# Two pacing tables of a two-layer transformer step changed: when VectorE gathers the w_ada products in the feed-forward stage, and how densely layer 0's weight sums are made in DRAM

## The chip, the cores and the metric

The kernel runs on one core of a Trainium2 chip. A core has a matrix engine (TensorE: PE in the profile, with its weight loads shown apart as PEld), VectorE (DVE), ScalarE (ACT), GpSimd (POOL) and SyncE (SP), which here only issues DMA transfers. Each engine works through its own instructions in order and waits on semaphores for the others; 16 DMA engines move data between DRAM and on-chip memory. The metric is the device time of one execution in microseconds (us).

## The reference, cut to what matters

Two trunk layers are run over 640 tokens (128 context, 512 latent), with model width 1024 and feed-forward width 2816, all in float32.

```python
def trunk_layer(x, mod, ...):
    sh1, sc1, g1, sh2, sc2, g2 = jnp.split(mod, 6, axis=-1)     # mod = silu(c) @ w_ada[l] + b_ada[l]
    h = rms_norm(x, g_pre[0]) * (1 + sc1) + sh1
    qa, ka, va, qb, kb, vb, uc, gates = combined_projection(h, w_in_l)
    oa, ob = attend(qa, ka, va, qb, kb, vb)
    oc = fourier_mix(uc)
    y = merge_branches(oa, ob, oc, gates, w_branch_l, w_out_l)  # sigmoid(gate) * (o @ w_branch), summed, @ w_out
    x = x + g1 * rms_norm(y, g_post[0])
    h = rms_norm(x, g_pre[1]) * (1 + sc2) + sh2
    x = x + g2 * rms_norm(swiglu(h, w_ffn_in_l, w_ffn_out_l), g_post[1])
```

`mod` needs, for each layer, a product of one vector with the 1024 x 6144 matrix `w_ada[l]`; its six parts are needed at different places, and the kernel computes them as six "rounds".

## The kernel before, in words

**Weights.** Every weight tile (512 KB: 128 x 1024 floats) is loaded by SP into one of 4 `wraw` buffers (`pump`, L168; halves for pairs of products L164) and then split into two float32r parts: ACT writes `whi` (L172), DVE writes `wlo`, the rest (L173). A product is three matmuls: hi by hi, hi by lo, lo by hi. SP takes the loads in order, each as soon as a buffer comes free.

**A planned clock.** The program is written out by hand in one order. `vt` adds up the planned TensorE time of what has been written so far (columns at 2.4 GHz; real time is longer, as the attention's own work is not counted). `step(dur)`, called after each product, writes side work into the program when `vt` has reached its time: the DRAM sums, the w_ada steps and the attention ticks. So two tables decide where in each engine's order the side work stands; nothing is decided at run time.

**The stages of a layer.** First the projections, Fourier mixing and attention; then the gates of branch B with the last merges (`merge(1, n)`), where TensorE also computes w_ada rounds (`ADA_MIX`: three rounds in layer 0, two in layer 1; weights through the same 4 `wraw` buffers, L492); then `out_proj`; then the feed-forward (`ffn`) in three parts of 6, 8 and 8 column blocks. Each part is a run of **pairs** (4, 8 and 8 of them) and then an **output product**. A pair (`pair`) computes two column blocks with seven half-size products (12 matmuls of 320 columns each). Its partial results leave PSUM through ACT (L750, L758) and DVE (L754, L764, L768, L773) into three `tmp` buffers, which ACT, DVE and POOL (L765) work on; then the gate function runs (L1536 to L1542). The output product (`xstat`; L1397 to L1399) multiplies the activations by `w_ffn_out`, one 512 KB unit after another: 6 units in part 1, 8 in part 2, 30 matmuls of 512 columns each; results are gathered on ACT in part 1 (L1578) and on DVE in part 2 (L1580). Part 3 ends in another form, `xstat_tiles`.

**w_ada in the feed-forward.** Four rounds in layer 0 and one in layer 1 run here on DVE (`ada_round` with `acc`). A round has 8 loads of 512 KB into three `ada_side` buffers (SP, L153; the next load is written right behind the step that frees its buffer) and 16 DVE steps over 128 x 1024 floats (L498 for the first load, L500 after that), two per load; then three empty steps (`ADA_LAG`), and a last one in which TensorE adds up over partitions (L512). `step` writes one DVE step each time `ada_acc` has gathered `ada_dt`.

**Sums in DRAM.** The half-size products need four sums of blocks of `w_ffn_in`, made wholly in DRAM (`sum_jobs`): 96 jobs a layer, each over 256 rows. Copies go through SP (L412), additions through POOL's DMA queue (L415), and a copy of a sum waits for the addition before it. Job i of layer 0 is written at planned time `SUM_START + i * SUM_DT[0]`; layer 1's jobs are paced by `SUM_DT[1]` from layer 0's feed-forward on.

Of the kernel before, what the change touches and what calls it, by code (L numbers as in the profile page):

```python
# [34 lines left out]
ADA_FFN = ([(0, 5), (1, 0), (1, 1), (1, 2)], [(1, 5)])  # L35
FFN_PARTS = (6, 8, 8)
SUMS_AT = (0.1, 0.2, 2.0, 3.0, 4.0, 5.0, 9.0, 99.0)
SUM_START, SUM_DT, SUM_ROWS = 20.0, (3.6, 7.5), 256
TICK = 2.5
ADA_DT, ADA_LAG = 4.2, 3  # L40
T_TOK, T_KO, T_V = 2.7, 0.9, 2.9
ADA_D0 = 2.1
T_COL, T_OUT, T_GM = 8.0, 5.2, 2.0
# [244 lines left out]
class Kernel:  # L288
# [1221 lines left out]
    def ffn(self, l):  # L1510
        nc = self.nc
        n0 = 0
        while self.sums_due:
            self.sums_due.popleft()()
        if l + 1 < L:
            self.sums_due, self.sums_at, self.sums_dt = deque(self.sum_jobs(l + 1)), self.vt, SUM_DT[1]
        for p, nt in enumerate(FFN_PARTS):
            last = p == len(FFN_PARTS) - 1
            aT = [self.fp.tile([128, 4, T], F32R, name=f"aT{i}", tag=f"mt{i}", bufs=1) for i in range(4)]

            def split_of(j, aT=aT):

                return tuple(aT[i + j // 4][:, j % 4, :] for i in (0, 2))

            def lhs(j, t, split_of=split_of):
                return tuple(self.cut(w, t) for w in split_of(j))
            gate = {}

            def evac(kind, n, gate=gate, split_of=split_of, n0=n0):
                def f(src, g):  # L1530
                    c0, c1 = HALVES[g]
                    if n not in gate:
                        gate[n] = self.fp.tile([128, T], F32, name="sg", tag="sg", bufs=2)
                    t = gate[n][:, c0:c1]
                    if kind == "fg":
                        nc.scalar.activation(t, src, AF.Tanh, scale=0.5)  # L1536
                        nc.vector.scalar_tensor_tensor(t, t, 1.0, src, op0=OP.add, op1=OP.mult)
                        return
                    nc.vector.tensor_tensor(t, t, src, op=OP.mult)  # L1539
                    hi, lo = (w[:, c0:c1] for w in split_of(n - n0))  # L1540
                    nc.scalar.activation(hi, t, AF.Copy, scale=0.5)
                    nc.vector.scalar_tensor_tensor(lo, t, 0.5, hi.bitcast(F32), op0=OP.mult, op1=OP.subtract)  # L1542
                return f

            first = n0
            if p == 0:
                first = FFN_SINGLE
                seq = [(kind, n) for n in range(first) for kind in ("fg", "fu")]
                self.tmp = [self.fp.tile([128, 320], F32, name=f"tmp{i}") for i in range(3)]
                for g in range(2):  # L1550
                    self.run_tasks(GTOK[g])
                    if g:
                        self.sums(self.z, SUMS_AT)
                    for kind, n in seq[:3]:
                        self.proj((l, kind, n), g, evac(kind, n), 4, HALVES)
                self.W.alt.clear()
                for kind, n in seq[3:]:
                    self.proj2((l, kind, n), evac(kind, n), HALVES)
                self.run_tasks(("sums",))
                rounds = ADA_FFN[l]  # L1560
                self.run_tasks(range(5))
                side = self.fp.tile([128, 5, D], F32, name="ada_side", tag="x", bufs=1)
                self.W.side_open([side[:, i, :] for i in range(2, 5)], 8 * len(rounds))
                self.ada = self.ada_rounds(rounds, side[:, 0:2, :])
                self.ada_acc, self.ada_dt = 0.0, ADA_DT
            half = (n0 + nt - first) // 2
            for n in range(first, first + half):
                for kind in ("fg", "fu"):
                    ev = [evac(kind, n + i * half) for i in range(2)]
                    self.pair(("pair", l, kind, n, n + half), lambda i, src, g: ev[i](src, g))  # L1570
            if p == 0:
                y = self.fix.tile([128, 5, D], F32, name="y", tag="os", bufs=1)
            keys = [[((l, "fo", h, n0 + k), k) for k in range(0, nt, 2)] for h in range(2)]
            if not last:
                def acc_y(t, h, ps, p=p):
                    d = y[:, t, 512 * h:512 * h + 512]
                    if p == 0:
                        nc.scalar.activation(d, ps, AF.Copy)  # L1578
                    else:
                        nc.vector.tensor_tensor(d, d, ps, op=OP.add)  # L1580
                self.xstat(keys, lhs, acc_y)
            else:
                self.ada_finish()
                self.alt_pieces()
                gm = self.load_gm(l, 1)
                self.x = self.fp.tile([128, 5, D], F32, name="x", tag="x", bufs=1)
                for t in range(5):
                    nc.sync.dma_start(self.x[:, t, :], self.xmid[t * 128:t * 128 + 128])

                def done(t, h, ps):  # L1590
                    c = slice(512 * h, 512 * h + 512)
                    d = y[:, t, c]
                    nc.vector.tensor_tensor(d, d, ps, op=OP.add)
                    self.square(t, h, d)

                    def scale():
                        (nc.vector if h else nc.gpsimd).tensor_tensor(d, d, gm[:, min(t, 1), c], op=OP.mult)
                    if h == 0 and t in GTOK[1]:
                        self.defer(T_GM, scale, ("gm", t))
                    else:  # L1600
                        scale()
                    if h == 1:
                        self.run_tasks((("gm", t),))
                        self.tail(l + 1, 0 if l + 1 < L else None, t, y[:, t, :])
                self.xstat_tiles(keys, lhs, done)
            n0 += nt
# [129 lines left out]
```

## Time and profile before

| | |
|---|---|
| Time, median of 3 runs | 2187.17 us (2185.57 to 2188.48) |
| Profiled execution: its own time | 2188.79 us |
| Profiled execution: span from first to last instruction | 2187.0 us |
| Busy share of the span | PE 96%, PEld 89%, DVE 58%, ACT 42%, POOL 23% |
| Mean granted TensorE clock (1 is 2.4 GHz) | 0.992 |

TensorE is nearly always busy, so time is saved only where it waits or where its clock is low. The other engines' shares are means over stages that differ.

### The profile page before, as it was taken

The page shows a single profiled execution, that of the slowest core. Times are in us where ns is not written, and L with a number is a line of the kernel's source. Part 1 is how long each engine was busy: PE and PEld are TensorE (multiplying, and loading weights), DVE is VectorE, ACT ScalarE, POOL GpSimd, SP SyncE. Part 2 cuts the span into 40 slices and gives each one's busy share as a digit, 9 for nine tenths or more (in the row PEclk, how much of TensorE's full clock was granted, in tenths as well). Part 3 has the DMA queues.
Part 4 walks back from the last instruction along what each step waited for, and adds up shares of the span by engine and source line. Part 5 has one row for each costly group of instructions (what it writes and reads, how often), then busy time and mean ns, then how long its engine had stood idle before and what let it go on. Part 6 is the DMA issues. An engine that isn't in the chain of part 4 may idle for free.

```text
span 2187.0 us, 36116 instructions
## 1 busy us (share of the span) xinstructions
PE 2109.1 (96%) x13876; PEld 1944.0 (89%) x13876; DVE 1272.2 (58%) x2377; ACT 910.0 (42%) x1944; POOL 510.8 (23%) x783
## 2 busy tenths in 40 slices
PE   6999999999899998999999999999999999999998
PEld 4999999998778888889879999999989898998996
DVE  3555565552247858668765556555433687573773
ACT  3644444432245344324345544434323543441451
POOL 3112335432224111102142112243321320010012
PEclk9999999999899999999999999999999999999999
DMA  7443477778864767668856334555565344442443
GB/s 271 137 97 89 110 177 191 176 190 251 237 205 138 211 178 200 179 198 222 248 165 161 88 96 104 132 131 128 130 184 203 124 136 143 123 150 86 135 149 121
DMA packets 369804, 349.69 MB, mean 160 GB/s; under 512 B 16608, under 2 KB 294144, under 8 KB 369376
## 3 DMA queue, kind: packets, MB, share of 16 engines
q1 hardware_dynamic: 337040, 293.51, 42.6%
q0 software_dynamic: 32160, 53.63, 14.9%
q8 instruction: 109, 1.79, 0.3%
q14 instruction: 63, 0.52, 0.1%
q10 hardware_dynamic: 432, 0.25, 0.0%
HBM read 335.50 MB, written 95.72 MB: 197 GB/s over the span
## 4 chain that ended last, share of the span: by engine, by line
PE 55%; DVE 7%; ACT 3%; issue 3%; DMA 1%; POOL 1%; DVEq 0%; ACTq 0%; SPq 0%; POOLq 0%
PE ps_mm L741 15%; PE ps_mm L647 7%; PE ps_mm L648 6%; PE ps_mm L649 6%; PE ps_mm L1397 5%; PE ps_mm L1398 5%; PE ps_mm L1399 5%; PE ps_o L849 1%; DVE wlo L173 1%; DVE ada_side L500 1%; PE ps_t L836 1%; ACT whi L172 1%; DVE sg L1539 1%; PE ps_s L809 1%; PE ps_s L810 1%
## 5 line engine op out<-in xcount | busy, mean ns | idle before, releaser
L173 DVE TENSOR_TENSOR wlo<-wraw,whi 128x512 fp32r<-128x512 f32 (+1 forms) x453 | 405.7, 901 | 394.5 <-ACT whi L172 389.2
L647 PE MATMUL ps_mm<-hT_hi,whi 128*128 128x256 f32 (+2 forms) x1552 | 491.8, 317 | 11.7 <-ACT whi L172 10.1
L649 PE MATMUL ps_mm<-hT_hi,wlo 128*128 128x256 f32 (+2 forms) x1552 | 483.5, 312 | 2.8 <-DVE wlo L173 2.8
L648 PE MATMUL ps_mm<-hT_lo,whi 128*128 128x256 f32 (+2 forms) x1552 | 483.0, 311 | 0.0
L172 ACT ACTIVATE whi<-wraw 128x512 fp32r<-128x512 f32 (+1 forms) x453 | 354.0, 790 | 305.6 <-PE ps_mm L1399 126.5
L647 PEld LDWEIGHTS ps_mm<-hT_hi,whi 128*128 128x128 f32 x1552 | 294.3, 190 | 22.2 <-ACT whi L172 12.5
L649 PEld LDWEIGHTS ps_mm<-hT_hi,wlo 128*128 128x128 f32 x1552 | 293.9, 189 | 4.9 <-DVE wlo L173 4.9
L648 PEld LDWEIGHTS ps_mm<-hT_lo,whi 128*128 128x128 f32 x1552 | 294.2, 190 | 0.4
L741 PE MATMUL ps_mm<-S,whi 128*128 128x320 f32 x960 | 214.1, 311 | 8.1 <-DVE tmp L754 8.1
L741 PE MATMUL ps_mm<-hT_hi,whi 128*128 128x320 f32 x640 | 199.8, 312 | 14.7 <-ACT tmp L750 14.7
L741 PE MATMUL ps_mm<-hT_hi,wlo 128*128 128x320 f32 x640 | 198.5, 310 | 0.0
L741 PE MATMUL ps_mm<-hT_lo,whi 128*128 128x320 f32 x640 | 198.4, 310 | 0.0
L765 POOL TENSOR_TENSOR tmp<-tmp,tmp 128x320 f32<-128x320 f32 x40 | 52.9, 1323 | 590.7 <-DVE tmp L764 482.9
L741 PEld LDWEIGHTS ps_mm<-S,whi 128*128 128x128 f32 x960 | 160.5, 189 | 11.3 <-DVE tmp L754 11.2
L1397 PE MATMUL ps_mm<-whi,aT 128*128 128x512 f32 x400 | 158.2, 395 | 0.0
L1399 PE MATMUL ps_mm<-whi,aT 128*128 128x512 f32 x400 | 157.9, 395 | 0.0
L1398 PE MATMUL ps_mm<-wlo,aT 128*128 128x512 f32 x400 | 157.8, 394 | 0.0
L741 PE MATMUL ps_mm<-S,wlo 128*128 128x320 f32 x480 | 148.3, 309 | 0.0
L741 PEld LDWEIGHTS ps_mm<-hT_hi,whi 128*128 128x128 f32 x640 | 120.9, 189 | 19.0 <-ACT tmp L750 17.3
L741 PEld LDWEIGHTS ps_mm<-hT_lo,whi 128*128 128x128 f32 x640 | 121.0, 189 | 0.1
L741 PEld LDWEIGHTS ps_mm<-hT_hi,wlo 128*128 128x128 f32 x640 | 121.1, 189 | 0.0
L1333 ACT ACTIVATE sg<-ps_mm 128x384 f32<-128x384 f32 x96 | 41.7, 435 | 190.3 <-PE ps_mm L649 190.2
(236 smaller groups left out, 3998.9 us busy)
## 6 DMA issues: line engine op xcount, KB each, us to landing
wraw<-in_w_in SPq DMA_DIRECT2D x92, 512.0 KB, 4.7
wraw<-wsum SPq DMA_DIRECT2D x160, 256.0 KB, 3.4
wsum<-in_w_ffn_in POOLq DMA_DIRECT2D x64, 512.0 KB, 6.9
wraw<-in_w_ffn_in SPq DMA_DIRECT2D x120, 256.0 KB, 3.8
wraw<-in_w_ada SPq DMA_DIRECT2D x56, 512.0 KB, 6.1
wraw<-in_w_ffn_out SPq DMA_DIRECT2D x44, 512.0 KB, 3.6
ada_side<-in_w_ada SPq DMA_DIRECT2D x40, 512.0 KB, 4.8
wsum<-in_w_ffn_in SPq DMA_DIRECT2D x32, 512.0 KB, 5.2
```

The lines of the kernel that those rows point to most:

```text
L172: self.k.nc.scalar.activation(hi, src, AF.Copy)
L173: self.k.nc.vector.tensor_tensor(lo, src, hi.bitcast(F32), op=OP.subtract)
L500: nc.vector.scalar_tensor_tensor(acc[:, s, :], u.raw, c, acc[:, s, :], op0=OP.mult, op1=OP.add)
L647: nc.tensor.matmul(ps, wh, xh[:, c0:c1], start=(k == 0), stop=False)
L648: nc.tensor.matmul(ps, wh, xl[:, c0:c1], start=False, stop=False)
L649: nc.tensor.matmul(ps, wl, xh[:, c0:c1], start=False, stop=(k == K - 1))
L741: nc.tensor.matmul(ps, w[p][:, k, :], x[q][:, k, :], start=first and k == 0 and j == 0, stop=last and k == 3 and j == 2, skip_group_check= ...
L765: nc.gpsimd.tensor_tensor(m5, m5, m1, op=OP.subtract)
L1333: lambda ps, g: self.nc.scalar.activation(sg[:, GROUPS[g][0]:GROUPS[g][1]], ps, AF.Tanh, scale=0.5))
L1397: nc.tensor.matmul(ps, xh, u.hi[:, i, :], start=st and i == 0, stop=False)
L1398: nc.tensor.matmul(ps, xh, u.lo[:, i, :], start=False, stop=False)
L1399: nc.tensor.matmul(ps, xl, u.hi[:, i, :], start=False, stop=sp and i == 1)
```

## The change

Layer 0's sums start at planned time 5.0 and come every 2.9, where they started at 20.0 and came every 3.6. A w_ada step in the feed-forward is written every 8.0 of planned time in the pairs and every 1.8 in the output products of parts 1 and 2, where it was every 4.2 throughout.

```diff
-SUM_START, SUM_DT, SUM_ROWS = 20.0, (3.6, 7.5), 256
+SUM_START, SUM_DT, SUM_ROWS = 5.0, (2.9, 7.5), 256
 TICK = 2.5
-ADA_DT, ADA_LAG = 4.2, 3
+ADA_DT, ADA_LAG = (8.0, 1.8), 3
...
-                self.ada_acc, self.ada_dt = 0.0, ADA_DT
+                self.ada_acc, self.ada_dt = 0.0, ADA_DT[0]
...
+                self.ada_dt = ADA_DT[1]
                 self.xstat(keys, lhs, acc_y)
+                self.ada_dt = ADA_DT[0]
```

Worked out from the tables: the last of layer 0's sums was written at planned time 363, after the gates and last merges (293 to 357), and now at 284, ahead of them.

**VectorE in a pair** (layer 0, part 2, the second pair). Rows from the middle of it, before; `tmp`, `sg` and `aT` are the pair's own tiles, `wlo` a weight split, `ada_side` a w_ada step:

```order
L173 TENSOR_TENSOR wlo_272<-wraw,whi_271 128x512
L500 SCALAR_TENSOR_TENSOR ada_side<-ada_side,ada_st 128x1024
L173 TENSOR_TENSOR wlo_272<-wraw,whi_271 128x512
L1539 TENSOR_TENSOR sg<-sg,ps_mm 128x320
L1542 SCALAR_TENSOR_TENSOR aT_7803<-sg,aT_7801 128x320
L173 TENSOR_TENSOR wlo_270<-wraw,whi_269 128x512
L764 TENSOR_TENSOR tmp_6661<-ps_mm,tmp_6661 128x320
L173 TENSOR_TENSOR wlo_270<-wraw,whi_269 128x512
L500 SCALAR_TENSOR_TENSOR ada_side<-ada_side,ada_st 128x1024
L768 TENSOR_TENSOR tmp_6662<-ps_mm,tmp_6662 128x320
```

The same place of the changed kernel:

```order
L173 TENSOR_TENSOR wlo_272<-wraw,whi_271 128x512 x2
L500 SCALAR_TENSOR_TENSOR ada_side<-ada_side,ada_st 128x1024
L1539 TENSOR_TENSOR sg<-sg,ps_mm 128x320
L1542 SCALAR_TENSOR_TENSOR aT_7826<-sg,aT_7824 128x320
L173 TENSOR_TENSOR wlo_270<-wraw,whi_269 128x512
L764 TENSOR_TENSOR tmp_6661<-ps_mm,tmp_6661 128x320
L173 TENSOR_TENSOR wlo_270<-wraw,whi_269 128x512
L768 TENSOR_TENSOR tmp_6662<-ps_mm,tmp_6662 128x320
```

Of two steps in these rows one is left. Over the eight pairs of part 2 the steps that work on DVE go from 18 to 8.

**VectorE at the end of part 2's output product** (layer 0), its last two units and the start of the first pair of part 3; `y` rows gather the product's results. Before:

```order
L173 TENSOR_TENSOR wlo_272<-wraw,whi_271 128x512 x2
L500 SCALAR_TENSOR_TENSOR ada_side<-ada_side,ada_st 128x1024
L1580 TENSOR_TENSOR y<-y,ps_mm 128x512 x5
L173 TENSOR_TENSOR wlo_270<-wraw,whi_269 128x512 x2
L500 SCALAR_TENSOR_TENSOR ada_side<-ada_side,ada_st 128x1024 x2
L173 TENSOR_TENSOR wlo_268<-wraw,whi_267 128x512
L754 TENSOR_TENSOR tmp_6661<-ps_mm,tmp_6662 128x320
```

The same place of the changed kernel:

```order
L500 SCALAR_TENSOR_TENSOR ada_side<-ada_side,ada_st 128x1024 x3
L1580 TENSOR_TENSOR y<-y,ps_mm 128x512 x5
L173 TENSOR_TENSOR wlo_270<-wraw,whi_269 128x512 x2
L500 SCALAR_TENSOR_TENSOR ada_side<-ada_side,ada_st 128x1024 x4
L173 TENSOR_TENSOR wlo_268<-wraw,whi_267 128x512
L754 TENSOR_TENSOR tmp_6661<-ps_mm,tmp_6662 128x320
```

Three steps instead of one stand ahead of the last gathering, and four instead of two ahead of the first pair's L754. At the first unit of part 1's output product six stand in a row, elsewhere in the output products two to four.

**SyncE in the gates of layer 0** (a piece of the difference; `wsum` rows are the DRAM sums):

```order
 L168 DMA wraw<-in_w_in 128x8x128
 L168 DMA wraw<-in_w_ada 128x1024 x3
-L412 DMA wsum_97<-wsum_96 256x512
-L168 DMA wraw<-in_w_branch 128x4x256
-L168 DMA wraw<-in_w_ada 128x1024
-L412 DMA wsum_97<-wsum_96 256x512
+L168 DMA wraw<-in_w_branch 128x4x256
+L168 DMA wraw<-in_w_ada 128x1024
 L168 DMA wraw<-in_w_in 128x8x128
 L168 DMA wraw<-in_w_ada 128x1024 x2
```

The copies are gone from here; they, and POOL's additions with them, stand further ahead, among the attention's loads. Between the weight loads nothing else moved.

## Rows read from the trace of the kernel before

**Rows 1.** The page: busy time, share of the span and instructions.

```profile
PE 2109.1 (96%) x13876; PEld 1944.0 (89%) x13876; DVE 1272.2 (58%) x2377; ACT 910.0 (42%) x1944; POOL 510.8 (23%) x783
```

**Rows 2.** Waits of PEld, whole run: us in total, times, longest.

```profile
PEld ps_mm L741 <- ACT tmp L750: 17.3, 10, 3.2
...
PEld ps_mm L741 <- DVE tmp L754: 11.2, 12, 1.1
```

**Rows 3.** Waits of PEld in layer 0's gates, 503.21 to 601.8 us.

```profile
PEld ps_mm L647 <- ACT whi L172: 10.7, 3, 3.9
...
PEld ps_mm L649 <- DVE wlo L173: 3.0, 4, 1.0
```

**Rows 4.** Windows, gates: length; PE, PEld, DVE, ACT, POOL busy; clock; DMA share; GB/s.

```profile
503.21:601.80 98.59, 87.45 (x627) 73.29 (x628) 23.60 (x39) 20.04 (x35) 22.73 (x32) 0.93 0.87 252
...
1601.01:1677.20 76.19, 75.42 (x564) 67.13 (x565) 23.06 (x39) 19.84 (x35) 15.35 (x20) 1.00 0.60 180
```

**Rows 5.** Timeline, PEld in layer 0's gates: start, length, instruction, [idle before].

```profile
548.19 0.19 PEld L647 LDWEIGHTS ps_mm<-hT_hi,whi 128*128 128x128 f32 x1 [3.92 <-ACT whi L172]
...
586.70 0.29 PEld L647 LDWEIGHTS ps_mm<-hT_hi,whi 128*128 128x128 f32 x1 [3.28 <-ACT whi L172]
```

**Rows 6.** Timeline, SP in layer 0's gates.

```profile
540.24 0.38 SPq L168 DMA_DIRECT2D wraw<-in_w_in  x1
...
555.73 0.38 SPq L168 DMA_DIRECT2D wraw<-in_w_in  x1
```

**Rows 7.** Timeline, ACT in layer 0's gates.

```profile
547.08 1.06 ACT L172 ACTIVATE whi<-wraw 128x1024 fp32r<-128x1024 f32 x1 [7.75 <-DMA wraw<-in_w_in]
...
566.25 1.06 ACT L172 ACTIVATE whi<-wraw 128x1024 fp32r<-128x1024 f32 x1 [11.05 <-DMA wraw<-in_w_in]
```

**Rows 8.** The page: DMA issues: count, KB each, median us to landing.

```profile
wraw<-in_w_in SPq DMA_DIRECT2D x92, 512.0 KB, 4.7
```

**Rows 9.** Windows of low clock, columns as in Rows 4.

```profile
548.45:551.87 3.42, 2.97 (x10) 2.46 (x10) 1.74 (x3) 0.53 (x1) 1.85 (x2) 0.50 0.47 143
...
586.00:592.83 6.83, 5.88 (x17) 5.37 (x18) 3.00 (x4) 1.98 (x3) 0.47 (x1) 0.50 0.53 202
...
1022.90:1026.32 3.42, 3.42 (x13) 3.42 (x14) 3.27 (x6) 1.82 (x4) 0.00 (x0) 0.50 0.53 155
```

**Rows 10.** Windows: part 1's output product, pairs and output product of part 2, layer 0; part 2's pairs, layer 1.

```profile
753.10:796.00 42.90, 42.90 (x198) 34.13 (x196) 19.75 (x23) 14.31 (x22) 5.96 (x10) 1.00 0.65 173
796.00:908.10 112.10, 103.17 (x695) 100.81 (x692) 91.98 (x150) 48.16 (x99) 17.24 (x19) 0.98 0.68 191
908.10:963.90 55.80, 55.80 (x242) 45.25 (x242) 32.74 (x39) 10.78 (x14) 3.13 (x4) 1.00 0.64 179
...
1869.60:1968.20 98.60, 98.60 (x676) 98.56 (x673) 71.99 (x130) 49.06 (x99) 10.73 (x8) 1.00 0.49 145
```

**Rows 11.** DVE groups in layer 0's second output product: count, busy us, mean ns, idle before.

```profile
L500 DVE SCALAR_TENSOR_TENSOR ada_side<-ada_side,ada_st 128x1024 f32<-128x1024 f32 x11 | 13.8, 1278 | 0.0
L173 DVE TENSOR_TENSOR wlo<-wraw,whi 128x1024 fp32r<-128x1024 f32 x6 | 7.4, 1225 | 12.1 <-ACT whi L172 12.1
L1580 DVE TENSOR_TENSOR y<-y,ps_mm 128x512 f32<-128x512 f32 x9 | 5.9, 683 | 2.1 <-PE ps_mm L1399 2.1
```

**Rows 12.** Timeline, DVE where layer 0's part 3 begins.

```profile
965.86 2.47 DVE L500 SCALAR_TENSOR_TENSOR ada_side<-ada_side,ada_st 128x1024 f32<-128x1024 f32 x2
...
968.86 0.48 DVE L754 TENSOR_TENSOR tmp<-ps_mm,tmp 128x320 f32<-128x320 f32 x1
```

**Rows 13.** Tile ada_side, 690 to 1140 us: duration ns min/median/max, first and last start.

```profile
L500 DVE SCALAR_TENSOR_TENSOR ada_side<-ada_side,ada_st x56: 1272/1279/1902, 717.9 to 1067.6; 128x1024 f32<-128x1024 f32 x56
...
DMA to landing us min/median/max: 3.4/4.8/7.0
```

**Rows 14.** Waits of ACT's weight splits in layer 0's attention, 257.45 to 503.21 us.

```profile
ACT whi L172 <- PE ps_mm L648: 11.1, 5, 2.5
```

**Rows 15.** Waits of SP's queue, whole run.

```profile
SPq L412 <- DMA wsum<-in_w_ffn_in: 4.5, 2, 3.1
```

## The prediction

> **What bounds the kernel now.** I read the page first: TensorE is busy 96% of the span [rows 1], so only its waits and the stretches of low clock can be won back. The waits of its weight loads (PEld) show best what a wait costs, since the matmul's own end is modelled. Nearly all waits after the start lie in two places that this change touches.
>
> The first is the gates of layer 0. There TensorE waits three times for ACT's split of a weight tile, 10.7 us, and behind each for DVE's half of it, 3.0 us in all [rows 3]; the first and the last of the three are 3.92 and 3.28 us [rows 5]. ACT itself waits for the load [rows 7]: the tile issued at 540.24 was split at 547.08, 6.8 us later, the one issued at 555.73 at 566.25, 10.5 us later [rows 6, 7], where such a load takes 4.7 us in the median of the run [rows 8]. So the transfer is late, not an engine. The DMA engines are 87% busy there; the same stage in layer 1, which has no DRAM sums in it and one w_ada round less, has them 60% busy, and takes 76.19 us instead of 98.59 [rows 4]. After each wait the granted clock falls to 0.50 (1.2 GHz): stretches of 3.42, 3.42 and 6.83 us, of which the first and the last stand in [rows 9].
>
> The second is the pairs. In the whole run they wait 17.3 us for ACT's copy of a partial result (L750) and 11.2 us for DVE's sum of two (L754) [rows 2], 28.5 us in all, and two further stretches of 3.42 us at clock 0.50 follow such waits (the later one in [rows 9]). They come with the w_ada steps: layer 1's eight pairs of part 2 have none and take 98.60 us, 12.3 each, without a stall, with DVE 71.99 us busy, 9.0 a pair. The same eight in layer 0 take 112.10 us with DVE 91.98 us busy [rows 10]. ACT's L750 writes a buffer that DVE read last in the pair before, so both kinds of wait are a late DVE.
>
> **The change, part by part.**
>
> *Sums earlier.* The last sum now stands ahead of the gates; their transfers there go. What is left there is what layer 1 has, and one more w_ada round. I take the median landing of 4.7 us for the gate loads in place of 6.8 and 10.5. The first wait then shrinks by 2.1 us to 1.8; the second load comes 5.8 us sooner, more than its wait of 3.5 (10.7 less the other two); the third I take like the second. DVE's half falls from 3.0 to 1. So 13.7 us of waits become 2.8. The low clock lasted 13.67 us, of which matmuls filled 2.97 of the first 3.42 and 5.88 of the last 6.83 [rows 9], about 12.3 in all; it cost half of that, 6.1; I keep 0.8 for one fall that may follow the first wait half of the time. Gain 13.7 + 6.1 - 2.8 - 0.8 = 16.2, less 1 because a third round keeps the queue fuller than in layer 1: **15**. Bounds: 0, if the w_ada loads alone make the gate loads late, and 19.
>
> What the earlier sums meet is hidden: in the attention from 257 to 503 us, where sums already run at the old pace, no weight split waited for a load, only for TensorE to free a slot, 5 times, 11.1 us [rows 14]. With 24% more sums a second that cover shrinks, but it is several tiles deep. SP's copies waited for an addition only twice, 4.5 us [rows 15]. I put 0 for it.
>
> *Fewer steps in the pairs.* A step takes 1.28 us [rows 13]. Part 2's pairs keep 8 of 18 steps in layer 0, so DVE needs about 9.0 + 1.3 us a pair instead of 9.0 + 2.5 in 12.3; part 3's and part 1's pairs lose as much or more. At up to two steps in a pair I expect a wait now and then where a step stands right ahead of L754: 2.5 us in all. Gain 28.5 - 2.5 = 26, and two low-clock stretches at half of 3.42: 3.4. Together **29.4**. Bounds: 14 (half of the waits stay, as where a step stands counts more than how many there are) and 32.
>
> *More steps in the output products.* TensorE did not wait in either output product: 42.90 and 55.80 us, fully busy [rows 10]. A unit takes 7.0 us there (55.80 over 8). DVE's work in one is a split, 1.2, and three to four steps of 1.28 [rows 11]: 5.0 to 6.3 us, and 3.4 more in the two units whose five results it gathers at 0.68 each. It fits, with little to spare; the first burst of six (7.7 us) runs over by 2 and is made up by the next, of three. Splits are three units ahead, so a lag of some us hides.
>
> It does not hide at the end, where the last burst stands ahead of the next pair's L754. That must be done before the pair's fifth product, 4 x 1.76 = 7.0 us after the pair begins (12.3 over seven products). Part 3 began at 963.90 [rows 10] and L754 at 968.86, behind two steps that took 2.47 [rows 12]. Two more steps stand there now, and two more ahead of the last gathering, which ends about 1.2 us later for them (2.5 less the gaps in it, 2.1 over nine gatherings [rows 11]; an estimate). L754 then ends at 968.9 + 0.5 + 2.5 + 1.2 = 973.1, against 963.9 + 7.0 = 970.9: a wait of **2.2**, and half of the time a fall of the clock, **0.8**. At part 2's start no gathering is on DVE (part 1 uses ACT); four steps instead of one lighter one make a wait of **0.5**. Layer 1's round is over before its output product ends: 0.
>
> *The loads of these steps.* In the first output product some seven more `ada_side` loads of 512 KB fall into 42.90 us, where DMA is 65% busy at 173 GB/s [rows 10]: 3.7 MB, 86 GB/s more, in proportion 0.32, so about 0.97. In the second likewise 0.64 + 0.24 = 0.88. A load has about 7 us from its issue until DVE needs it (one unit, with three buffers); now it takes 4.8 us, at most 7.0 [rows 13]. Some will be late, by a us or two, and DVE holds the delay until the pair: I put **2** for both ends together; bounds 0 and the first rival below.
>
> The Trainium skill (DMA: Bandwidth & Descriptors, Queues, rings and completion order) says that every DMA engine takes turns, packet by packet, between the queues that have work. By that rule a side load on SP's queue that meets an addition on POOL's queue goes at half its rate for as long, and if each met one from end to end, 4.8 us would become 9.6 and the sum some 16 us worse. The trace has them overlap without that: 7.0 at most.
>
> **The sum.** 15 + 29.4 - 2.2 - 0.8 - 0.5 - 2 = 38.9 us. The profiled span of 2187.0 becomes 2148.1. The profiled execution took 1.8 us more than its span, 2188.79, and 1.6 more than the median of 2187.17; I take the same sum off the median: 2148.3, rounded to **2148**.
>
> **The rivals.**
>
> *Late side loads* (12%). The output products become DMA-bound. If the loads take there what gate loads took at 87% busy, 6.8 to 10.5 us, one load a unit is late by about 2 us, DVE makes up 0.5 of it, and the lag at the pairs is 1.5 x 5 = 7.5 and 1.5 x 6 = 9 us, all of it a stall, with two falls of the clock, 3.4. That is 19.9 in place of the 2: 2148 + 18 = 2166. For it: 0.97. Against it: a late load puts off the next request too, so the queue doesn't grow, and layer 1's additions can be late without harm.
>
> *The gates stay starved* (12%). Three w_ada loads stand ahead of each gate load on SP, and they, not the sums, may set the landing. Then the gain is 5 instead of 15: 2158. For it: layer 1 still has waits there, if under 2 us. Against it: layer 1's 60%.
>
> *Half of the pairs' waits stay* (10%). 14 in place of 29.4: 2163. For it: the 22 waits [rows 2] came from more than three times as many steps (56 L500 in layer 0 alone [rows 13]), so most steps cost nothing already, and the costly places may be among those that stay. Against it: DVE's busy time in layer 0's pairs, which the fewer steps bring near that of layer 1.
>
> *Slower* (4%). The denser sums stop SP: copies that read a sum stand two jobs, 5.8 us of planned time, behind its addition, and SP is in order, so a weight load behind a stopped copy is late. Layer 0 has 24 such copies. It decides at 1.8 us of unhidden wait in each (24 x 1.8 = 43, the gain and the 4 us below); at 2.5 us it would be 60 - 38.9, a loss of 21: 2208. Against it: two waits, 4.5 us, at the old pace [rows 15].
>
> **How the numbers follow.** Forecast 62%, alone 2139 to 2156. The cases of less gain reach to 2166, and two of them together lie beyond; on the other side all waits gone would be 2187 - 19 - 32 = 2136. Range 2136 to 2169, which leaves out the slower rival and mixtures past 2169. A measurement here tells 0.2%, about 4 us, from no change. Faster holds the forecast and the three smaller gains, less a little for several of them at once: 0.92; same 0.03; slower 0.05.
>
> **What would show it.** Gates of layer 0 at 80 to 85 us with DMA share below 0.75 and clock near 1.00. Part 2's pairs of layer 0 near 100 us. Output products still 42.9 and 55.8. The first pair of part 3 with a wait of 2 to 3 us for L754. The attention of layer 0 as long as before. I am wrong if DVE waits for `ada_side` loads in the output products, if gate splits still wait for loads by 3 us, or if the attention grows.

## The result, and the profile after

The changed kernel takes 2161.65 us in the median of 4 runs (2158.87 to 2163.07), the kernel before 2186.37 us on the same chip (2184.34 to 2188.48, 4 runs): a ratio of 0.9878 (0.9864 to 0.9893). It is 24.7 us faster. The forecast was 2148 us, its range 2136 to 2169.

The profiled execution is the fastest of the four, 2158.87 us with a span of 2157.1 us: 29.9 us less than the profiled one of before. Of these, 2.8 us (2161.65 - 2158.87) and 2.4 us (2188.79 - 2186.37) are only the place of the two executions among their runs. The page's first row after, to be held against [rows 1]:

```profile
PE 2097.4 (97%) x13876; PEld 1936.5 (90%) x13876; DVE 1273.7 (59%) x2377; ACT 911.1 (42%) x1944; POOL 511.3 (24%) x783
```

The waits of weight loads (PEld) after, whole run: us in total, times, longest.

```profile
PEld ps_s L809 <- DVE sm L811: 11.4, 10, 6.7
...
PEld ps_mm L741 <- DVE tmp L754: 7.4, 7, 1.6
...
PEld ps_mm L741 <- ACT tmp L750: 2.7, 4, 0.8
```

The pairs' 28.5 us [rows 2] are down to 10.1. But the first row has grown: TensorE waits 11.4 us for the softmax of the attention (DVE, L811), where before it was 2.1. The windows say the same by stage: layer 0's attention, its gates, part 1's output product, part 2's pairs and output product (columns as in [rows 4]).

```profile
56.72:514.75 458.03, 447.16 (x3286) 428.61 (x3286) 251.98 (x579) 206.59 (x493) 146.64 (x250) 0.99 0.68 164
514.75:595.17 80.42, 80.41 (x628) 68.36 (x629) 21.92 (x37) 19.38 (x35) 15.23 (x23) 1.00 0.63 208
740.94:783.92 42.98, 42.98 (x199) 34.16 (x198) 31.63 (x36) 13.38 (x20) 6.03 (x9) 1.00 0.78 212
783.92:887.98 104.06, 101.04 (x691) 99.16 (x690) 83.57 (x143) 49.42 (x100) 17.47 (x19) 1.00 0.71 199
887.98:945.11 57.13, 57.13 (x261) 45.67 (x260) 44.04 (x52) 10.50 (x14) 6.67 (x10) 1.00 0.74 214
```

The gates are at 80.4 instead of 98.6 us [rows 4], fully busy, DMA share 0.63, clock 1.00; part 2's pairs at 104.1 instead of 112.1 [rows 10]. The second output product is 1.4 us longer (57.13 after 55.68, measured between the same two weight loads; the bounds in [rows 10] are rounded), because 16 of TensorE's own small w_ada matmuls (L512) and what follows them moved into it (x261 after x242), out of the pairs of part 3; it is fully busy. The attention is the loser. Its window before:

```profile
57.45:503.21 445.76, 443.78 (x3286) 427.18 (x3286) 251.84 (x579) 205.96 (x493) 138.59 (x240) 1.00 0.61 147
```

The same 3286 matmuls take 12.3 us more, with 9 us more of waiting and a fall of the clock. Since TensorE's order is the same in both kernels up to the first output product, each weight load can be held against itself: the changed kernel runs ahead by 0.7 us at 44 us and by 0.3 at 300 us, falls to 2.2 us behind at 306 us and, from 2.6 behind at 407 us, to 10.7 behind at 422 us; nowhere else in the attention does it lose 1 us. So there are two places, and they have the same form. The earlier one, on POOL and then on DVE (start, length, engine, line; idle before, and what ended it):

```profile
278.00 0.91 POOL L415 DMA_DIRECT2D wsum<-in_w_ffn_in  x1 [13.05 <-DMA wsum<-wsum]
```

```profile
301.31 0.56 DVE L811 CUSTOM_DVE_ANT_0 P<-ps_s,bias 128x384 f32<-128x384 f32 x1 [1.41 <-POOL bias L1218]
```

The later one costs more. On POOL after:

```profile
379.14 1.29 POOL L415 DMA_DIRECT2D wsum<-in_w_ffn_in  x1
396.53 0.87 POOL L415 DMA_DIRECT2D wsum<-in_w_ffn_in  x1 [16.09 <-DMA wsum<-wsum]
...
400.78 1.74 POOL L1203 MEMSET klo<- 64x896 f32 x2
...
403.15 2.40 POOL L1211 DMA_DIRECT2D bias<-in_b_rpbT  x4
...
416.33 5.13 POOL L1218 TENSOR_TENSOR bias<-bias,colmask 128x256 f32<-128x256 f32 x6 [6.50 <-DMA bias<-in_b_rpbT]
```

An addition (L415) stands on POOL ahead of everything that prepares the attention's next bias: clearing buffers (L1203), loading it (L1211), masking it (L1218). The addition waits 16.1 us for the copy that it adds to. That copy is SP's, and SP was held at a weight load until 390.9:

```profile
380.80 10.01 SPq L168 DMA_DIRECT2D wraw<-in_w_in  x2
390.91 0.54 SPq L412 DMA_DIRECT2D wsum<-wsum  x1
```

DVE then waits for the bias, and TensorE for DVE:

```profile
417.08 0.56 DVE L811 CUSTOM_DVE_ANT_0 P<-ps_s,bias 128x384 f32<-128x384 f32 x1 [6.56 <-POOL bias L1218]
```

```profile
417.70 0.29 PEld L809 LDWEIGHTS ps_s<-khi,qst 128*128 128x128 f32 x1 [6.74 <-DVE sm L811]
```

The granted clock is 0.50 (1.2 GHz) around it, in a stretch with 4.04 us of matmuls:

```profile
415.96:422.78 6.82, 4.04 (x11) 3.54 (x12) 2.30 (x5) 0.12 (x1) 6.45 (x9) 0.50 0.08 21
```

Before, the additions that stood there waited for no copy, and the mask was done at 405.3 us (398.61 + 6.70), 3.8 us before L811 began at 409.12; that was the reserve. POOL before:

```profile
376.08 2.80 POOL L415 DMA_DIRECT2D wsum<-in_w_ffn_in  x3
...
380.58 1.74 POOL L1203 MEMSET klo<- 64x896 f32 x2
...
398.61 6.70 POOL L1218 TENSOR_TENSOR bias<-bias,colmask 128x256 f32<-128x256 f32 x6 [7.17 <-DMA bias<-in_b_rpbT]
```

That POOL works strictly in its own order is what the rows show (none of its other work runs in the 16.1 us of the wait), and what the Trainium skill says of GpSimd's queue (PSUM — Partial Sum Buffer, Engine vs sequencer instructions).

### The profile page after: what moved, and what is told of

Same layout as the page of the kernel before. It is cut to its first block, busy times and chain, and to the rows that moved or that the text cites. A ratio compares the mean times of both kernels' runs of the same rounds, so it can differ in the third digit from the quotient of the medians.

```text
span 2157.1 us, 36129 instructions
## 1 busy us (share of the span) xinstructions
PE 2097.4 (97%) x13876; PEld 1936.5 (90%) x13876; DVE 1273.7 (59%) x2377; ACT 911.1 (42%) x1944; POOL 511.3 (24%) x783
## 3 DMA queue, kind: packets, MB, share of 16 engines
q0 software_dynamic: 32160, 53.63, 14.9%
## 4 chain that ended last, share of the span: by engine, by line
PE 60%; DVE 3%; issue 2%; ACT 2%; POOL 1%; DMA 1%; DVEq 0%; POOLq 0%; ACTq 0%
PE ps_mm L741 21%; PE ps_mm L647 7%; PE ps_mm L648 7%; PE ps_mm L649 7%; PE ps_mm L1397 5%; PE ps_mm L1399 5%; PE ps_mm L1398 5%; PE ps_o L849 1%; PE ps_t L836 1%; PE ps_s L809 1%; PE ps_s L810 1%; POOL hT_lo L628 1%; ACT whi L172 1%; DVE wlo L173 0%; DVE ada_side L500 0%
## 5 line engine op out<-in xcount | busy, mean ns | idle before, releaser
L649 PEld LDWEIGHTS ps_mm<-hT_hi,wlo 128*128 128x128 f32 x1552 | 292.3, 188 | 2.5 <-DVE wlo L173 2.5
L647 PE MATMUL ps_mm<-o,whi 128*128 128x256 f32 (+1 forms) x384 | 121.3, 316 | 0.0
```

The lines of the kernel that those rows point to most:

```text
L647: nc.tensor.matmul(ps, wh, xh[:, c0:c1], start=(k == 0), stop=False)
L649: nc.tensor.matmul(ps, wl, xh[:, c0:c1], start=False, stop=(k == K - 1))
```

## The experiments

Each ran beside the kernel before on the same chip (median of before there: 2189.45 us for sums_alone to denser, 2189.86 for two_chains to steps_not_at_part_start, 2190.87 for the last three). The stages are read from the one profiled execution of each kernel, between the same weight loads of TensorE; the first two rows are the two kernels of the prediction.

| kernel | median us | ratio to before (95%) | layer 0: attention, gates, pairs of parts 1, 2, 3 |
|---|---|---|---|
| before | 2186.37 | | 445.8, 98.6, 55.7, 112.0, 109.5 |
| the changed kernel | 2161.65 | 0.9878 (0.9864 to 0.9893) | 458.0, 80.4, 50.4, 104.1, 102.8 |
| sums_alone | 2185.14 | 0.9978 (0.9968 to 0.9987) | 456.8, 80.5, 55.6, 111.9, 109.6 |
| steps_alone | 2165.97 | 0.9891 (0.9878 to 0.9905) | 446.1, 95.7, 52.1, 104.1, 102.7 |
| six_chains | 2150.25 | 0.9822 (0.9809 to 0.9836) | 446.7, 80.4, 52.4, 104.0, 102.7 |
| denser | 2179.25 | 0.9954 (0.9942 to 0.9967) | 474.5, 80.5, 52.4, 104.1, 102.7 |
| two_chains | 2151.91 | 0.9827 (0.9813 to 0.9842) | 449.1, 80.4, 51.1, 104.1, 102.7 |
| steps_mid_pair | 2148.95 | 0.9818 (0.9803 to 0.9833) | 446.3, 80.5, 49.4, 106.0, 101.0 |
| steps_first_product | 2168.32 | 0.9899 (0.9883 to 0.9916) | 445.6, 80.5, 50.8, 104.0, 100.0 |
| steps_not_at_part_start | 2153.03 | 0.9838 (0.9823 to 0.9853) | 446.2, 80.4, 49.8, 103.5, 103.5 |
| steps_by_kind | 2153.23 | 0.9827 (0.9813 to 0.9840) | 445.7, 81.0, 52.0, 101.3, 101.9 |
| steps_by_kind_inverse | 2168.36 | 0.9891 (0.9878 to 0.9905) | 445.9, 80.4, 51.5, 114.3, 110.1 |
| steps_by_kind_early_end | 2148.36 | 0.9809 (0.9796 to 0.9823) | 446.4, 80.9, 53.2, 103.0, 99.8 |

**The two edits apart.** sums_alone:

```diff
-ADA_DT, ADA_LAG = (8.0, 1.8), 3
+ADA_DT, ADA_LAG = (4.2, 4.2), 3
```

> The sums' new pacing with the w_ada steps at the old 4.2 throughout. Theory A (the layer 0 attention pays: POOL stops at an addition whose copy is late, and the attention's bias work is queued behind it): gates of layer 0 at about 80 us instead of 98.6 (-18), attention at about 458 us instead of 446 (+12), pairs as before; net about -6, 2180 us, ratio 0.997. Rival B (the two edits are not independent: the attention's loss is a matter of one execution, and the sums alone bring nearly the whole 15 us forecast): 2171 us, ratio 0.993.

steps_alone:

```diff
-SUM_START, SUM_DT, SUM_ROWS = 5.0, (2.9, 7.5), 256
+SUM_START, SUM_DT, SUM_ROWS = 20.0, (3.6, 7.5), 256
```

> The w_ada steps at 8.0 and 1.8, the sums at the old pace. Theory A (edits independent): attention 446 us, gates 98.6 us, the four groups of pairs together 22 us shorter, output products within 2 us of before; 2186 - 22 = 2164 us, ratio 0.990. Rival: the pairs' gain needs the calmer queues that the early sums leave; then 2170 us or more.

Both came out by theory A: 0.2% for the sums, 1.1% for the steps, and together 1.2%. The sums cut the gates by 18 us and lengthen the attention by 11 in the same kernel; each stage answers almost wholly to one edit. Without the early sums the gates stay starved (steps_alone, window of the gates: clock 0.95, DMA share 0.88), so it was the sums, not the w_ada loads, that made the gate loads late (columns as in [rows 4]):

```profile
506.23:601.91 95.68, 85.92 (x628) 71.90 (x628) 23.59 (x39) 19.93 (x35) 22.49 (x32) 0.95 0.88 257
```

**Is it the order on POOL, or the traffic?** six_chains writes the same jobs at the same planned times, with the six chains of sums side by side, so that an addition stands 12 jobs or more behind its copy, and so does a copy of a sum behind its addition:

```diff
-                for ops in steps:
-                    for op, out, src in ops:
-                        for r in rows:
-                            yield op(out, src, r)
+                chains.append([[op(out, src, r) for op, out, src in ops for r in rows] for ops in steps])
...
+        if l == 0:
+            chains = [[sum(s, []) for s in zip(*chains)]]
+        for k in chains:
+            for s in k:
+                yield from s
```

> The changed kernel, the same 96 jobs of layer 0 at the same planned times, but the six chains of sums written side by side, so that an addition stands 12 jobs or more behind its copy instead of 2. Theory A (POOL stopped at additions that wait for their copy): the waits of 13 and 16 us on POOL are gone, the bias is ready in time, attention back to about 446 us, gates still 80; 2161.6 - 12 = 2150 us, ratio to before 0.983. Rival C (the denser transfers as such make the attention's loads late, whatever their order): attention still about 458 us, 2161 us.

two_chains does so for two chains at a time (4 jobs of distance):

> The changed kernel with the chains of the two kinds side by side, two at a time: an addition stands 4 jobs (11.6 of planned time) behind its copy instead of 2. Theory A: SP holds a copy for up to about 11 us behind weight loads, so most of POOL's waits of 13 and 16 us go, but not all; attention 447 to 452 us, 2150 to 2156 us. Rival C (transfers as such) is then already out or in by the six chains; this one gives the distance that is needed.

denser keeps the old order at a faster pace:

```diff
-SUM_START, SUM_DT, SUM_ROWS = 5.0, (2.9, 7.5), 256
+SUM_START, SUM_DT, SUM_ROWS = 5.0, (2.4, 7.5), 256
```

> The changed kernel with layer 0's sums every 2.4 instead of 2.9. Theory A: an addition stands 4.8 of planned time behind its copy instead of 5.8, so more of them stop POOL; but it costs only where the stop stands ahead of a bias round, so the attention may be anything from 450 to 475 us; gates still 80; 2155 to 2180 us. Rival C (transfers as such): the attention grows with the density, to about 468 us; 2171 us. The rival 'slower' of the prediction (SP stops at copies): over 2186 us.

POOL's waits in the attention for the copy of a sum (us, times, longest): the changed kernel, denser, and two_chains, whose lines are one further down. In six_chains no addition waits for a copy.

```profile
POOL wsum L415 <- DMA wsum<-wsum: 38.3, 7, 16.1
```

```profile
POOL wsum L415 <- DMA wsum<-wsum: 78.6, 7, 17.4
```

```profile
POOL wsum L416 <- DMA wsum<-wsum: 8.4, 2, 7.6
```

The attention follows these waits: 446.7, 449.1, 458.0 and 474.5 us for 0, 8.4, 38.3 and 78.6. It does not follow the traffic: six_chains moves data at the highest rate of the four, 168 GB/s (147 before), and its attention is within 1 us of that before:

```profile
57.98:504.72 446.74, 444.75 (x3286) 427.10 (x3286) 252.88 (x579) 206.32 (x493) 148.86 (x250) 1.00 0.70 168
```

Rival C falls. denser shows the direction that the "slower" rival feared, though it stays below the time before. There SP's copies wait for additions too, 54.9 us in its attention (7.7 in the changed kernel, none in six_chains and two_chains), and whatever stops a copy makes the addition behind it later. So the runs do not part POOL's stops from SP's: six chains end both. What they do show is the way by which TensorE is reached. No load of weights got late by it: in denser ACT's splits wait 1.0 us for one, as in the changed kernel, while DVE waits 14.9 us for POOL's mask, where the changed kernel has 9.5 and six_chains nothing. The first three lines are of denser's attention, the last of the changed kernel's:

```profile
SPq L412 <- DMA wsum<-in_w_ffn_in: 54.9, 8, 15.0
ACT whi L172 <- DMA wraw<-in_w_in: 1.0, 1, 1.0
DVE P L811 <- POOL bias L1218: 14.9, 6, 4.6
```

```profile
DVE P L811 <- POOL bias L1218: 9.5, 3, 6.6
```

denser has the same start of the sums as the changed kernel and only a faster pace, so pace alone adds to the stops; what the earlier start (5.0 instead of 20.0) does by itself was not run.

**Where a step stands in a pair.** What was left to win was in the pairs: 10.1 us of waits. steps_mid_pair lets a step be written only behind products 3 to 6 (all of the following have the six chains too):

```diff
         def end(i):
             W.part_done(key, i)
+            self.ada_ok = i in (2, 3, 4, 5)
             self.step(12 * 320 * PE_COL)
+            self.ada_ok = True
...
-        while self.ada is not None and self.ada_acc >= self.ada_dt:
+        while self.ada is not None and self.ada_acc >= self.ada_dt and self.ada_ok:
```

> Six chains, and in a pair a w_ada step may be written only behind products 3 to 6 (one that falls due behind product 7, 1 or 2 waits for product 3). Theory A (the place decides: a step behind product 1 or 2 runs into L754 of the same pair, one behind 3 to 6 has room): of the 10.1 us of waits left in the pairs only those at the starts of parts 2 and 3 stay, 2.8 us; 2150 - 7 = 2143 us, ratio to before 0.979. Rival B (the number decides: DVE is short of time in these pairs): waits only move to other pairs, 2150 us.

The opposite, `i == 0`, is steps_first_product:

> The opposite: in a pair a step may be written only behind product 1, with nearly the same number of steps in the pairs (21 instead of 24 in layer 0). Theory A (place): every pair with a step waits 1.7 us or more (0.6 for L750 and 1.1 for L754 in the two clean cases after the change), the 12 pairs of layer 0 that have one or two about 25 us in place of the 7 of such pairs; 2150 + 18 = 2168 us or more with falls of the clock. Rival B (number): 2150 us. The output products begin with bursts of 10 and 9 steps, which by the prediction's sum they make up within two units.

steps_not_at_part_start is steps_mid_pair with `ada_ok` off behind the last unit of an output product:

> As steps_mid_pair, and no step behind the last unit of an output product (the steps that stood there go to the next part's pairs and the last four rounds end at the end of part 3's pairs). Theory A: the waits of 1.6 and 1.25 us in the first pairs of parts 2 and 3 go as well, if the two steps behind products 3 and 6 fit; 2143 - 3 = 2140 us. Rival B (number): the eight more steps in pairs bring new waits, 2145 us or more.

None of the three went as theory A had it. On balance steps_mid_pair took 5.5 us of waits out of the pairs, but among those left is a wait of 2.3 us that came with a fall of the clock in part 2, the output product behind it grew by 1.3 us, and its time cannot be told from that of six_chains. steps_first_product met its 2168 us for another reason: its pairs did not wait more (104.0 and 100.0 us), a single step behind product 1 cost 0.6 us at most, two in a row up to 2.1, and the loss is in the output products (48.2 and 67.5 us), where the bursts of 10 and 9 steps made TensorE wait for DVE before its own sums over partitions. Nor were its steps in layer 0's pairs nearly as many: by the order on DVE 11 worked there, 17 in six_chains, so number and place changed together. In the stretch from its first output product to the start of part 3 (L515 and L503 are L512 and L500 of the changed kernel):

```profile
PEld ps_t L515 <- DVE ada_side L503: 8.6, 4, 3.3
...
PEld ps_t L515 <- issue: 3.9, 3, 3.3
```

steps_not_at_part_start freed the first pairs of parts 2 and 3 of their waits, as expected, but with the steps that moved into them layer 0's other pairs wait 9.3 us for L750 (L755 there), where steps_mid_pair has 2.9.

So "behind product 1 or 2" was the wrong rule. Read pair by pair, though, the changed kernel's remaining waits of over half a microsecond all stand in pairs that compute a gate (`fg`): two of them first in a part, one first in layer 1, and the other five right behind a pair that ends with the product of both (`fu`). steps_by_kind writes a step, one at a time, in `fg` pairs only behind products 3 to 6 and in `fu` pairs only behind 1 to 3; steps_by_kind_inverse does the opposite (1 to 3 in `fg`, 4 to 7 in `fu`). Both write 27 steps in layer 0's pairs, of which 22 and 21 work on DVE; the others are the empty ones and TensorE's sums. Both start the count anew at an output product and write every 7.0 in pairs. steps_by_kind_early_end is steps_by_kind with 5.6 and 1.6 and, as before, no step behind an output product's last unit:

```diff
+            self.ada_ok = int(i in ((2, 3, 4, 5) if key[2] == "fg" else (0, 1, 2)))
...
-                self.ada_dt = ADA_DT[1]
+                self.ada_acc, self.ada_dt = 0.0, ADA_DT[1]
```

> Six chains; a step at most once behind a product, in a gate pair (kind fg) only behind products 3 to 6, in the pair behind it (kind fu) only behind 1 to 3; every 7.0 in pairs, and the count starts anew at an output product, so its first unit gets three steps instead of six to eight. Layer 0's part 2 has 11 steps in its pairs. Theory A2 (a fu pair ends with DVE behind, as its two gate products and two splits come on top; a step late in a fu pair or early in the fg pair behind it runs into that pair's L750 and L754, a step elsewhere has room): only the waits in the first pairs of parts 2 and 3 stay, 3 us in all; part 2's pairs of layer 0 at 101 us or less; 2150 - 6 = 2144 us. Rival B (the number decides): 11 steps in part 2 wait as 10 did, about 104 us, and 2150 us.

> The same number of steps to within one a part (12 in part 2's pairs of layer 0), the same output products, but the other places: fg pairs only behind products 1 to 3, fu pairs only behind 4 to 7. Theory A2: every fg pair that follows a fu pair with steps waits 1.5 to 3 us, seven or eight of them in layer 0 and one in layer 1; part 2's pairs 104 to 110 us; 2155 to 2168 us with falls of the clock. Rival B (number): as steps_by_kind, within 3 us.

> As steps_by_kind, at 5.6 in pairs and 1.6 in output products, and no step behind the last unit of an output product. Theory A2: 16 steps in part 2's pairs fit still if places alone decide, and the first pairs lose their waits of 1.5 and 1.25 us too: 2141 us, and the pairs of part 2 at 98.5 to 99.5. Rival B (number): 16 steps wait more than 11, part 2's pairs 104 us or more, 2150 us or more. Output products at 1.6 (four steps a unit, 6.3 us with the split in a unit of 7.0) still fully busy.

Part 2's pairs of layer 0, steps_by_kind and then its inverse:

```profile
776.27:877.62 101.35, 99.83 (x674) 98.56 (x673) 84.17 (x141) 49.33 (x100) 14.67 (x14) 1.00 0.74 208
```

```profile
773.32:887.61 114.29, 105.70 (x690) 103.83 (x689) 86.39 (x140) 49.95 (x100) 15.32 (x16) 0.94 0.67 186
```

DVE is busy 84 and 86 us, but the inverse takes 13 us longer; over the three parts it is 255.2 against 275.8 us. So the same number costs 20.6 us more at other places: in the inverse six `fg` pairs wait for ACT's L750 (L756 there), and the granted clock falls to 0.50 at four of them:

```profile
PEld ps_mm L745 <- ACT tmp L756: 15.6, 6, 3.6
```

ACT is late because L756 stands in its order behind the last work of the `fu` pair (L1547; L1541 in the changed kernel), which waits for DVE's product (L1545), and that stood behind the steps. ACT around the first of these waits that is over 3 us long:

```profile
805.75 0.47 ACT L1547 ACTIVATE aT<-sg 128x320 fp32r<-128x320 f32 x1 [2.88 <-DVE sg L1545]
807.18 0.47 ACT L1547 ACTIVATE aT<-sg 128x320 fp32r<-128x320 f32 x1 [0.96 <-DVE sg L1545]
...
808.07 0.42 ACT L756 ACTIVATE tmp<-ps_mm 128x320 f32<-128x320 f32 x1
```

One rival is open: the inverse also puts up to three steps into one `fu` pair, steps_by_kind at most two into any pair, and no run parts the crowding from the kind of pair.

The number is not free either: with 16 steps in part 2 instead of 11, steps_by_kind_early_end needs 103.0 us there, not the 98.5 to 99.5 expected, and neither of the times of 2144 and 2141 us was reached. In part, what the places gained was lost elsewhere: steps_by_kind has output products of 46.9 and 59.3 us, in which TensorE again waited for DVE's steps (3.4 us, and a fall of the clock), where the inverse, at the same pace there, has 43.0 and 57.5 and steps_by_kind_early_end 43.0 and 57.1, all fully busy. The order says why. In steps_by_kind a round's last step, the empty ones and TensorE's sum (L516 there) fall into one burst, so that TensorE reaches the sum while DVE has still to do the last step; in the other two the sum stands a unit later. TensorE's weight loads and DVE's last step of that round in steps_by_kind:

```profile
757.62 0.16 PEld L516 LDWEIGHTS ps_t<-ada_side,ones 128*32 128x32 f32 x8 [0.36 <-issue]
760.33 0.17 PEld L516 LDWEIGHTS ps_t<-ada_side,ones 128*32 128x32 f32 x8 [2.56 <-DVE ada_side L504]
```

```profile
759.00 1.28 DVE L504 SCALAR_TENSOR_TENSOR ada_side<-ada_side,ada_st 128x1024 f32<-128x1024 f32 x1
```

In steps_by_kind_early_end the last step ended at 761.36 and the sum began at 763.0. The second output product of steps_by_kind is longer mainly because it holds two such sums instead of one (279 matmuls there, 261 in the changed kernel). The end result of the last one, 0.9809, is the best measured, but its interval overlaps that of six_chains, so what these steps in the pairs gained beyond six_chains is not shown.

## Why the prediction was right, and where it was not

The sign, the range and the order of the two gains held, but not the forecast itself: 2161.65 us lies outside its own 2139 to 2156, and what took the 12 us was none of the rivals of less gain. That the range still held is owed to the room that it left for those. Against the sum of the prediction, term by term:

- **Gates: 15 forecast, 18.2 measured** (98.59 to 80.41). All three waits went, and the clock never fell; the 1.8 + 1 us that I kept of them, the 0.8 for a fall and the 1 for the third w_ada round were not needed. What there was to win was less than I had, 19.8: TensorE stood idle for 11.1 us (98.59 - 87.45), as the 13.7 us of waits of weight loads ran in part beside a matmul, and its busy time fell by 7.0 (87.45 to 80.41) where I had 6.1 for the clock.
- **The earlier sums in the attention: 0 forecast, 12.3 lost.** This is the step that failed: "What the earlier sums meet is hidden ... I put 0 for it." I looked at splits that wait for loads [rows 14] and at SP's copies that wait for additions [rows 15]; the first stayed (10.6 us in five waits), the second grew to 7.7 us in three. I did not look at the third wait, POOL's additions that wait for SP's copies, and at what is queued behind them on POOL. A faster pace shortens the time between a copy and its addition from 7.2 to 5.8 of planned time, while SP holds a copy behind a weight load for 10 us. six_chains takes the stops between copies and additions away and lands at 0.9822; times the 2187.17 of before that is 2148.2, the forecast. That it is so to the microsecond is luck: without this term the others of the changed kernel add up to 42.1 us (18.2 + 21.4 + 2.5), 3.2 more than forecast.
- **Pairs and output products: 23.9 forecast, 21.4 measured.** The four groups of pairs gave 5.3, 7.9, 6.7 and 3.0 us, less the 1.4 that moved into the output product. Two errors cancel in part: of the waits in pairs 10.1 us stayed instead of 5.2 (the 2.5 for "now and then" was 7.3, because the place counts, as the rival "half of the pairs' waits stay" had it), and the 2 for late side loads and the 0.8 for the clock did not come. The reason given for the waits on L750, a buffer that DVE read last, is not what the rows show: L750 is late because it stands behind L1541 on ACT, as above. That a late DVE is at the root of both kinds of wait holds.
- **The starts of parts 2 and 3** (already in the line above): **2.7 forecast, 2.8 measured.** The agreement of the sums is luck: part 2 had 0.5 and took 1.56, part 3 had 2.2 and took 1.25. The first pair of part 3 shows the mechanism as described: L754 behind four steps, done at 953.47, 1.25 us late.

```profile
947.58 4.88 DVE L500 SCALAR_TENSOR_TENSOR ada_side<-ada_side,ada_st 128x1024 f32<-128x1024 f32 x4
952.37 0.70 DVE L173 TENSOR_TENSOR wlo<-wraw,whi 128x512 fp32r<-128x512 f32 x1
952.97 0.50 DVE L754 TENSOR_TENSOR tmp<-ps_mm,tmp 128x320 f32<-128x320 f32 x1
```

- **The rest, 2.5 gained**, is not from the change as far as is shown: 0.7 us of it lies ahead of the attention and 1.8 in layer 1 ahead of its feed-forward, where falls of the clock at the norms (1753.36 us before, 1105.45 after) come in one execution and not in another.

18.2 - 12.3 + 21.4 + 2.5 is the 29.9 us of the profiled executions, within rounding.

The rivals: *late side loads* is out, with a DMA share of 0.78 and 0.74 where I had worked out 0.97 and 0.88, since fewer loads fell into the output products than I took: in the first one 9 were issued after 4, five more and not seven, and 1.7 MB more were moved there (9.09 after 7.42), not 3.7. DVE waited for these loads twice, 1.4 us in all. The `ada_side` loads after, as in [rows 13]:

```profile
DMA to landing us min/median/max: 4.4/5.0/7.2
```

By the Trainium skill's rule (DMA: Bandwidth & Descriptors, Queues, rings and completion order) a load that shares its engines with an addition from end to end would have taken 9.6 us, an estimate from the median of 4.8; the slowest took 7.2, and no row here shows for how much of a load an addition ran beside it. *The gates stay starved* is out (sums_alone: 80.5). *Slower* had the right neighbourhood, a stop between copies and additions, but the wrong engine: no stop of SP for an addition is seen to make a weight load late (the splits' 1.0 us above), POOL's stops for a copy did reach TensorE.

## What to carry to other kernels

When side work with a chain of transfers is paced closer, list for every engine that issues it what waits for what, in both directions, and what stands behind each such wait in that engine's order; then look at how much time the first consumer behind it had to spare. Here it was under 4 us where the delay was 16, and 12 of 18 us won went back; writing independent chains side by side won them back at the same pace. Where small steps are spread over an engine that others wait for, their places, or their crowding in one pair, count as well as their number: 27 steps cost 20.6 us more in one arrangement than in another. And a sum that TensorE makes of DVE's result wants a stretch of other work between it and the last step (2.6 us here).

## What the runs showed of the hardware

That a burst on DVE can reach TensorE by a second way was not expected: not only by a late weight split or a late sum, but by TensorE's own small matmuls that read DVE's result (L512), which stand in order ahead of the output product's (8.6 us in four waits of steps_first_product).
